# A decoder layer on one core: leading phase staggered by one pair, last third sum on VectorE, odd partial sums added from PSUM

## The chip, the core and the metric

The kernel runs on one core of a Trainium2 chip. Five engines work side by side, each through its own instructions in order: TensorE (PE, matrix products), VectorE (DVE), ScalarE (ACT), GpSimd (POOL) and SyncE (SP, which here only issues transfers). Transfers (DMAs) are issued by an engine's queue and carried out by 16 DMA engines that all queues share. SBUF is the working memory, PSUM holds the matmuls' sums. The metric is the time of one execution in microseconds; lower is better.

## The reference

One decoder layer for 256 tokens of width 2048, all in float32: a half-step SwiGLU feed-forward block, a mixing block (differential attention beside an mLSTM, between one input and one output projection), a second half-step feed-forward block and a final norm. The feed-forward block is the part that the change touches most:

```python
def swiglu(h, w_gate, w_up, w_down):
    return (jax.nn.silu(h @ w_gate) * (h @ w_up)) @ w_down

x = x + 0.5 * swiglu(rmsnorm(x, ffn1_norm[l]), ffn1_w_gate[l], ffn1_w_up[l], ffn1_w_down[l])
...
x = x + jnp.concatenate([y_a, y_b], axis=-1) @ w_out[l]
x = x + 0.5 * swiglu(rmsnorm(x, ffn2_norm[l]), ffn2_w_gate[l], ffn2_w_up[l], ffn2_w_down[l])
```

The hidden width is 5632, that is 11 column blocks of 512.

## The kernel before

**Splitting.** Each float32 operand is split into a high and a low half of TensorE's own format: ACT casts the high half (`wh`, L131), VectorE subtracts it from the source to get the low half (`wl`, L132). A product of two operands is three matmuls: high by high, low by high (L178, L179), high by low (L181). Each weight is loaded, split on both engines, and used by TensorE. The tiles of split weights come from a pool of four, so ACT and VectorE can be up to four tiles ahead of TensorE.

**Sums in place of products.** Two weight matrices that share their input (gate and up, or two column blocks of a projection) run as one `Paired` run. For its first `ns` pairs of row blocks it uses a scheme of the Strassen-Winograd kind, seven products in place of eight, in which sums of weight blocks are multiplied by sums of input blocks. For each pair `j` a tile `raw` with three slots is loaded: slot 0 from the first matrix, slots 1 and 2 from the second (`load`, L412 to L421, two DMAs on POOL's queue, on SP's for the first runs). There are five such tiles. The rest of the rows (`rest`) is done plainly, in units of two row blocks (`plain`, 12 matmuls each).

A run has these phases:
- `leading` (L440): for each group of up to two pairs (`twos`), load; multiply slot 0 by A1 into bank `x`; then one VectorE instruction of 1024 columns makes two sums in place (L453); multiply the new slot 0 by S1 into bank `d`; then add slot 2 to slot 0, the third sum. The third sum is an accumulating DMA on POOL's queue (L460) in runs with `by_dma` set and more than three pairs, else a VectorE instruction (L462). The bank `x` is copied to the bank n11 by ACT (L469) behind the last A1.
- `sums` (L487): multiply the third sums (S2) into `x`; for each of them a second block of the first matrix (`late`) is loaded and added to slot 0 by an accumulating DMA (L496), and is multiplied by itself (`bare`); then S3.
- `second` (L522): the plain units of the first matrix and the products of the remaining sums; it ends the first result (`half`).
- `third` (L541): the plain units of the second matrix. It is a stream, taken by the next run during its `leading`; behind its last unit stands `end`, the use of the second result.

**Order.** `Chain.run` (L566) interleaves by hand: with three steps of the stream and three groups it takes a unit, the first group, a unit, the second group, the third group, the last unit, and then `end`. TensorE's order follows this. Splits, sums and loads are moved ahead by a priority (`AHEAD`), and the instructions that drain PSUM are placed at most a few splits later by `ahead_of_splits`.

**Feed-forward.** The hidden columns are done in parts of 3, 2, 3 and 3 blocks (`PARTS`). For each part come its up/gate runs (five pairs each, but for the first two runs of the kernel), then the down projection over the part's rows, as two runs, for column blocks (0, 1) and (2, 3), with 3, 1, 3, 3 pairs (`NP_DOWN`). For every part but the last the result is a partial sum that is added to the residual `xres`: `add(c)` (L615) calls `add_part` (L324), in which ACT scales it out of PSUM into a tile (L329) and POOL issues an accumulating DMA into `xres` (L330). Even `c` comes from `second`, odd `c` from `third`, whose `end` stands in the next run's leading phase. For the last part and for the output projection `residual` adds from PSUM on VectorE (L336).

In the notation used below, A01 is the A1 product of pairs 0 and 1, S23 the S1 product of pairs 2 and 3, A4 and S4 those of the single pair 4, and U1 to U3 the units of the stream.

Of the kernel before, what the change touches and what calls it, by code (L numbers as in the profile page):

```python
# [13 lines left out]
ALU = mybir.AluOpType  # L14
# [6 lines left out]
NT = S // P  # L21
# [3 lines left out]
CW = 512  # L25
# [17 lines left out]
AHEAD = 400  # L43
# [4 lines left out]
SLACK = 4  # L48
# [11 lines left out]
def tile_trunk_layer(ctx: ExitStack, tc: tile.TileContext, x, xt, par, bias_if, lamv, fnorm,  # L60
                     wg1, wu1, wd1, wqk0, wqk1, wqk2, win, wout, wg2, wu2, wd2, out):
    nc = tc.nc
# [14 lines left out]
    def nm(s):  # L77
        uid[0] += 1
        return f"{s}_{uid[0]}"
# [16 lines left out]
    def seeded(which):  # L96
        return ps_acc.tile([P, CW], F32, tag=f"acc{which}", name=nm(f"acc{which}"), bufs=1)
# [24 lines left out]
    xres = big.tile([P, NT, D], F32, name="xres")  # L122
# [21 lines left out]
    def ahead_of_splits(i, ins, slack=SLACK):  # L144
        queued[i].append((len(splits) + slack, ins))
# [154 lines left out]
    A1, B1, A2, B2, S3, S1, S2, S4 = range(8)  # L300
# [24 lines left out]
    def add_part(acc, hb, c):  # L325

        t = wk("part")
        with soon():
            ahead_of_splits(0, nc.scalar.activation(t, acc, AF.Copy, scale=0.5))  # L329
        nc.gpsimd.dma_start(xres[:, hb, c * CW:(c + 1) * CW], t, accum_op=ALU.add)  # L330

    def residual(accs, c, scale, parts):
        for hb in range(NT):
            xs = xres[:, hb, c * CW:(c + 1) * CW]
            with soon():
                ahead_of_splits(1, nc.vector.scalar_tensor_tensor(xs, accs[hb], scale, xs, op0=ALU.mult, op1=ALU.add))  # L336
        for hb in range(NT):
            square_sum(xres[:, hb, c * CW:(c + 1) * CW], parts[:, hb, c:c + 1])

# [18 lines left out]
    def wk(name):  # L358
        return work.tile([P, CW], F32, tag="w", name=nm(name))
# [11 lines left out]
    def soon(extra=40):  # L371
        return tc.high_priority(offset=AHEAD + extra)
# [17 lines left out]
    def aside(work):  # L390

        if work:
            work.pop(0)()

    class Paired:
# [44 lines left out]
        def leading(self):  # L440

            n = self.n
            self.x, self.d = bank()[:, 0:n], bank()[:, 0:n]
            for js in self.twos:
                for j in js:
                    self.load(j)
                self.part(js, self.x, A1, 0, True, True)
                if js[-1] == self.ns - 1:
                    self.n11 = self.copied(self.x, seeded(N11), SLACK - 2)
                with tc.high_priority(offset=AHEAD):  # L450
                    for j in js:
                        raw = self.raws[j]
                        nc.vector.tensor_tensor(out=raw[:, 0:2, :], in0=raw[:, 0:3:2, :],  # L453
                                                in1=raw[:, 1:2, :].to_broadcast([P, 2, n]), op=ALU.add)
                self.part(js, self.d, S1, 0, True, True)
                with tc.high_priority(offset=AHEAD):
                    for j in js:
                        raw = self.raws[j]
                        if self.by_dma:
                            nc.gpsimd.dma_start(raw[:, 0, :], raw[:, 2, :], accum_op=ALU.add)  # L460
                        else:
                            nc.vector.tensor_tensor(out=raw[:, 0, :], in0=raw[:, 0, :], in1=raw[:, 2, :], op=ALU.add)  # L462
                yield

        def copied(self, src, t, slack=SLACK - 1):

# [91 lines left out]
    class Chain:  # L558
# [7 lines left out]
        def run(self, p, half, end, last_units=1, lead=()):  # L566

            done = 0
            for f in lead:
                next(self.stream)  # L570
                done += 1
                f()
            q = len(p.twos)
            first = p.leading()
            for i in range(q):
                while done < min(self.steps - 1, -(-(i + 1) * self.steps // (q + 1))):
                    next(self.stream)
                    done += 1
                next(first)
                flush(1)  # L580
                aside(side)
            while done < self.steps:
                next(self.stream)
                done += 1
            next(first, None)
            self.end()
            p.sums()
            half(p.second())
            self.put(p.third(last_units), len(p.rest), lambda: end(p.accs()))
# [7 lines left out]
    def ffn(chain, xp, rstd, wg, wu, wd, finish, first=None):  # L597


        def inner(hid, c, ns):  # L600
            sg = []

            def half(ag):
                r = rstd()
                sg.extend(gate(ag[hb], r[:, hb:hb + 1]) for hb in range(NT))

            def end(au):
                r = rstd()
                with soon():
                    hs = [gated(au[hb], r[:, hb:hb + 1], sg[hb]) for hb in range(NT)]  # L610
                hid_transposes(hs, hid, c, ns)

            return half, end

        def add(c):  # L615
            return lambda accs: [add_part(accs[hb], hb, c) for hb in range(NT)]

        done = 0
        for part, (n, ns) in enumerate(zip(PARTS, NP_DOWN)):
            hid = {}  # L620
            for c in range(n):
                half, end = inner(hid, c, ns)
                if done + c == 0 and first is not None:
                    half(linear(xp, wg[0], KD, ahead=first[0], in_pieces=True,
                                banks=[functools.partial(seeded, b) for b in (N11, N21)]))
                    au = []
                    stream = units(au, xp, wu[0], KD, banks=[bank, bank])
                    for _ in range(KD // UK - NP):
                        next(stream)
                    chain.put(stream, NP, functools.partial(end, au))  # L630
                else:
                    np_, queue = NP, nc.sync if done + c < ON_POOL else nc.gpsimd
                    if done + c == 1 and first is not None:
                        np_ = NP_FIRST
                        pending.extend([first[1]] * (NP - NP_FIRST))
                    chain.run(Paired(xp, wg[done + c], wu[done + c], KD, np_, queue=queue), half, end)
            last = part == len(PARTS) - 1
            for c in (0, 2):
                p = Paired(hid, wd[c], wd[c + 1], n * 4, ns, done, by_dma=False)
                if last:  # L640
                    chain.run(p, functools.partial(finish, c), functools.partial(finish, c + 1),
                              LAST_UNITS if c else 1)
                else:
                    chain.run(p, add(c), add(c + 1))
            done += n
# [158 lines left out]
    accs = []  # L804
# [182 lines left out]
    for hb in range(NT):  # L987
        for h in range(NH):
            i = hb * NH + h
# [226 lines left out]
```

## Time and profile before

| | |
|---|---|
| median of 3 runs | 1792.17 us (1791.81 to 1792.82) |
| the profiled execution | 1793.79 us |
| its span, first to last instruction | 1792.1 us |
| granted TensorE clock | 0.998 |
| instructions | 24444 |
| VectorE, ACT, POOL busy | 1565.1, 1255.2, 456.2 us |
| accumulating DMAs: third sums L460, late L496, partial sums L330 | 112, 168, 48 |

A row of the table of groups reads: line, engine, operation, out<-in by tile names, shapes, count | busy us, mean ns of one | idle us of the engine just before them, and what ended most of it. A row of the table of stages reads: the stretch in us from the span's start and its length, then for each engine its busy us with the number of its instructions in brackets, then the granted clock, the mean busy share of the 16 DMA engines, and GB/s moved. A row of the timeline reads: start, duration, engine, line, operation, tiles, shapes, count [idle before <-what ended it]. A row of the waits reads: who waited on what: total us, times, longest us. DMA rows of the timeline show the issue, not the transfer.

### The profile page before, as it was taken

What the parts mean: (1) busy time and instruction counts of PE and PEld (TensorE: products, weight loads), DVE (VectorE), ACT (ScalarE), POOL (GpSimd) and SP (SyncE); (2) the same over time, 40 slices, a digit from 0 to 9 for tenths busy, and PEclk for the clock granted to TensorE, in tenths of its full rate; (3) what the DMA queues carried; (4) which work ended last, traced back from release to release, by engine and by line L of the source; (5) the groups of instructions that cost most, each with busy time, mean ns of one, the idle gap of its engine ahead of it and who ended that gap; (6) DMA issues with size and microseconds to landing.
All of it is one profiled execution on the core that took longest, in us unless ns stands there. A gap on an engine that the chain in (4) does not pass through costs nothing.

```text
span 1792.1 us, 24444 instructions
## 1 busy us (share of the span) xinstructions
PE 1768.2 (99%) x7954; PEld 1437.8 (80%) x7954; DVE 1565.1 (87%) x2090; ACT 1255.2 (70%) x1939; POOL 456.2 (25%) x653
## 2 busy tenths in 40 slices
PE   9999999999999999999999999999999999999997
PEld 6788878878887888987788788788878878887886
DVE  6888887899888999897788998998887899888997
ACT  7676666777676768776676777776776777676765
POOL 0022332333233321022221102132332333233310
PEclk9999999999999999999999999999999999999999
DMA  9887998999799986587776568997998999899974
GB/s 339 263 239 211 263 284 252 238 307 255 235 261 267 261 267 193 189 247 211 217 217 202 179 197 231 257 279 217 260 283 261 239 304 246 249 257 271 273 255 123
DMA packets 159552, 439.15 MB, mean 245 GB/s; under 512 B 18016, under 2 KB 19072, under 8 KB 159168
## 3 DMA queue, kind: packets, MB, share of 16 engines
q0 software_dynamic: 79952, 200.60, 46.6%
q1 hardware_dynamic: 78464, 234.90, 38.0%
q10 hardware_dynamic: 1008, 2.09, 0.3%
q8 instruction: 62, 1.02, 0.2%
q14 instruction: 66, 0.54, 0.1%
HBM read 349.56 MB, written 2.10 MB: 196 GB/s over the span
## 4 chain that ended last, share of the span: by engine, by line
PE 82%; DMA 6%; issue 4%; DVE 4%; ACT 2%; POOL 1%; SPq 0%; POOLq 0%; DVEq 0%; ACTq 0%
PE acc L181 16%; PE acc L178 15%; PE acc L179 15%; PE accn L178 11%; PE accn L179 11%; PE accn L181 11%; DMA raw<-in_wg_dram 4%; DVE wl L132 2%; DMA rawp<-in_wg_dram 1%; ACT wh L131 1%; DVE raw L453 1%; PE tr L346 1%; DMA raw<-raw 1%; POOL raw L460 0%; PE sc L1008 0%
## 5 line engine op out<-in xcount | busy, mean ns | idle before, releaser
L131 ACT CAST wh<-raw 128x512 fp32r<-128x512 f32 (+1 forms) x845 | 570.7, 707 | 269.8 <-DVE raw L453 156.1
L132 DVE TENSOR_TENSOR wl<-raw,wh 128x512 fp32r<-128x512 f32 (+1 forms) x845 | 646.0, 792 | 122.8 <-ACT wh L131 118.2
L132 DVE TENSOR_TENSOR wl<-rawp,wh 128x1024 fp32r<-128x1024 f32 (+3 forms) x324 | 384.2, 1198 | 49.2 <-ACT wh L131 43.7
L131 ACT CAST wh<-rawp 128x1024 fp32r<-128x1024 f32 (+3 forms) x324 | 330.1, 1034 | 64.0 <-PE accn L179 22.9
L178 PE MATMUL acc<-wh,xs 128*128 128x512 f32 (+2 forms) x904 | 351.8, 390 | 6.7 <-ACT wh L131 6.7
L179 PE MATMUL acc<-wh,xs 128*128 128x512 f32 (+2 forms) x904 | 349.6, 387 | 0.6 <-DVE xs L132 0.6
L181 PE MATMUL acc<-wl,xs 128*128 128x512 f32 (+2 forms) x904 | 305.4, 390 | 1.6 <-DVE wl L132 1.4
L496 POOL DMA_DIRECT2D raw<-late x168 | 150.5, 1032 | 390.6 <-DVE wl L132 340.3
L178 PE MATMUL acc<-wh,xt 128*128 128x512 f32 (+2 forms) x608 | 235.5, 388 | 0.4 <-ACT wh L131 0.4
L179 PE MATMUL acc<-wh,xt 128*128 128x512 f32 (+2 forms) x608 | 233.8, 386 | 0.0
L178 PE MATMUL accn<-wh,xt 128*128 128x512 f32 (+1 forms) x592 | 233.3, 398 | 0.0
L179 PE MATMUL accn<-wh,xt 128*128 128x512 f32 (+1 forms) x592 | 228.8, 390 | 0.0
L178 PEld LDWEIGHTS acc<-wh,xs 128*128 128x128 f32 x904 | 169.8, 188 | 45.6 <-ACT wh L131 11.8
L181 PEld LDWEIGHTS acc<-wl,xs 128*128 128x128 f32 x904 | 168.7, 188 | 46.4 <-DVE wl L132 12.4
L453 DVE TENSOR_TENSOR raw<-raw 128x1024 f32<-128x1024 f32 x168 | 199.8, 1216 | 2.1 <-DMA raw<-in_wu_dram 1.6
L179 PEld LDWEIGHTS acc<-wh,xs 128*128 128x128 f32 x904 | 169.8, 188 | 34.6 <-DVE xs L132 1.8
L460 POOL DMA_DIRECT2D raw<-raw x112 | 96.5, 864 | 328.3 <-DVE wl L132 286.6
L181 PE MATMUL acc<-wl,xt 128*128 128x512 f32 (+2 forms) x608 | 171.6, 390 | 0.5
L181 PE MATMUL accn<-wl,xt 128*128 128x512 f32 (+1 forms) x592 | 166.3, 389 | 0.0
L178 PE MATMUL accn<-wh,xs 128*128 128x512 f32 (+1 forms) x384 | 150.1, 392 | 2.4 <-ACT wh L131 2.4
L179 PE MATMUL accn<-wh,xs 128*128 128x512 f32 (+1 forms) x384 | 149.0, 389 | 0.0
L181 PEld LDWEIGHTS acc<-wl,xt 128*128 128x128 f32 x608 | 111.3, 188 | 30.0 <-DVE wl L132 9.0
(231 smaller groups left out, 2164.8 us busy)
## 6 DMA issues: line engine op xcount, KB each, us to landing
rawp<-in_wd_dram SPq DMA_DIRECT2D x96, 512.0 KB, 5.7
raw<-late POOLq DMA_DIRECT2D x166, 256.0 KB, 5.1
raw<-in_wu_dram POOLq DMA_DIRECT2D x80, 512.0 KB, 8.7
rawp<-in_wu_dram SPq DMA_DIRECT2D x74, 512.0 KB, 5.8
rawp<-in_wg_dram SPq DMA_DIRECT2D x70, 512.0 KB, 5.6
raw<-raw POOLq DMA_DIRECT2D x112, 256.0 KB, 4.6
rawp<-in_win_dram SPq DMA_DIRECT2D x44, 512.0 KB, 5.1
late<-in_wg_dram SPq DMA_DIRECT2D x41, 512.0 KB, 10.5
```

The costliest lines, as they stand in the source:

```text
L131: return (nc.scalar.copy(hi, src), nc.vector.tensor_tensor(out=lo, in0=src, in1=hi.bitcast(F32), op=ALU.subtract))
L132: nc.vector.tensor_tensor(out=lo, in0=src, in1=hi.bitcast(F32), op=ALU.subtract))
L178: nc.tensor.matmul(acc, lh, rh, start=first, stop=False, skip_group_check=on)
L179: nc.tensor.matmul(acc, ll, rh, start=False, stop=False, skip_group_check=on)
L181: nc.tensor.matmul(acc, lh, rl, start=False, stop=last, skip_group_check=on)
L346: nc.tensor.transpose(tr[:, i, hb * P:(hb + 1) * P], hs[hb][:, k * P:(k + 1) * P], ident)
L453: nc.vector.tensor_tensor(out=raw[:, 0:2, :], in0=raw[:, 0:3:2, :], in1=raw[:, 1:2, :].to_broadcast([P, 2, n]), op=ALU.add)
L460: nc.gpsimd.dma_start(raw[:, 0, :], raw[:, 2, :], accum_op=ALU.add)
L496: nc.gpsimd.dma_start(self.raws[j][:, 0, :], lates[-1][1][:, i, :], accum_op=ALU.add)
```

## The change

Three things are done.

The leading phase is staggered. In the pass of a group, A1 is multiplied and the two sums are made as before, but the S1 product and the third sum (`second_sum`) are those of the group before. The last group's follow when the generator is asked once more. `Chain.run` asks for that before the last step of the stream, where it asked after it.

In runs whose third sums are DMAs, those of the last group are VectorE instructions.

The partial sums of odd `c` are added to `xres` by VectorE straight from PSUM (`add_half`, taken out of `residual`); those of even `c` go by ACT and DMA as before.

```diff
+    def add_half(acc, xs, scale):
+        with soon():
+            ahead_of_splits(1, nc.vector.scalar_tensor_tensor(xs, acc, scale, xs, op0=ALU.mult, op1=ALU.add))
+
     def residual(accs, c, scale, parts):
         for hb in range(NT):
-            xs = xres[:, hb, c * CW:(c + 1) * CW]
-            with soon():
-                ahead_of_splits(1, nc.vector.scalar_tensor_tensor(xs, accs[hb], scale, xs, op0=ALU.mult, op1=ALU.add))
+            add_half(accs[hb], xres[:, hb, c * CW:(c + 1) * CW], scale)
...
-            for js in self.twos:
+            for i, js in enumerate(self.twos):
                 for j in js:
                     self.load(j)
                 self.part(js, self.x, A1, 0, True, True)
-                if js[-1] == self.ns - 1:
-                    self.n11 = self.copied(self.x, seeded(N11), SLACK - 2)
...
-                self.part(js, self.d, S1, 0, True, True)
-                with tc.high_priority(offset=AHEAD):
-                    for j in js:
-                        raw = self.raws[j]
-                        if self.by_dma:
-                            nc.gpsimd.dma_start(raw[:, 0, :], raw[:, 2, :], accum_op=ALU.add)
-                        else:
-                            nc.vector.tensor_tensor(out=raw[:, 0, :], in0=raw[:, 0, :], in1=raw[:, 2, :], op=ALU.add)
+                if i:
+                    self.second_sum(self.twos[i - 1])
+                if i == len(self.twos) - 1:
+                    self.n11 = self.copied(self.x, seeded(N11), SLACK - 2)
                 yield
+            self.second_sum(self.twos[-1])
+
+        def second_sum(self, js):
+
+            self.part(js, self.d, S1, 0, True, True)
+            with tc.high_priority(offset=AHEAD):
+                for j in js:
+                    raw = self.raws[j]
+                    if self.by_dma and js != self.twos[-1]:
+                        nc.gpsimd.dma_start(raw[:, 0, :], raw[:, 2, :], accum_op=ALU.add)
+                    else:
+                        nc.vector.tensor_tensor(out=raw[:, 0, :], in0=raw[:, 0, :], in1=raw[:, 2, :], op=ALU.add)
...
+            while done < self.steps - 1:
+                next(self.stream)
+                done += 1
+            next(first, None)
             while done < self.steps:
                 next(self.stream)
                 done += 1
-            next(first, None)
             self.end()
...
         def add(c):
-            return lambda accs: [add_part(accs[hb], hb, c) for hb in range(NT)]
+            def run(accs):
+                for hb in range(NT):
+                    if c % 2:
+                        add_half(accs[hb], xres[:, hb, c * CW:(c + 1) * CW], 0.5)
+                    else:
+                        add_part(accs[hb], hb, c)
+
+            return run
```

## The prediction, made before the changed kernel was run

> **What bounds the kernel now.** I read the page first, its engine shares and DMA queues, then the table of stages, then the timeline of single stretches.
>
> ```profile
> PE 1768.2 (99%) x7954; PEld 1437.8 (80%) x7954; DVE 1565.1 (87%) x2090; ACT 1255.2 (70%) x1939; POOL 456.2 (25%) x653
> DMA  9887998999799986587776568997998999899974
> q0 software_dynamic: 79952, 200.60, 46.6%
> q1 hardware_dynamic: 78464, 234.90, 38.0%
> ```
>
> PE looks full at 99%, VectorE has 227 us free, and the two DMA queues together hold 84.6% of the 16 engines. But a matmul is drawn longer than the step to the next one (0.40 us in a row below, against 0.22), so PE's busy share hides small stalls. The count of matmuls in windows of one length shows them. Here are nine windows of 18 us, each ending where the leading phase of an up/gate run ends: six in the second run after a change of part, then three in the third run, or in the second one after the output projection.
>
> ```profile
> core 0: us, PE busy (x) PEld busy (x) DVE busy (x) ACT busy (x) POOL busy (x), PEclk, DMA share, GB/s
> 230.30:248.30 18.00, 16.99 (x72) 12.74 (x71) 14.91 (x18) 8.91 (x14) 4.52 (x6) 1.00 1.03 343
> 357.40:375.40 18.00, 17.16 (x73) 12.91 (x72) 15.23 (x18) 9.18 (x14) 4.52 (x6) 1.00 1.05 358
> 547.20:565.20 18.00, 15.84 (x66) 11.54 (x64) 13.60 (x17) 7.79 (x14) 3.87 (x5) 1.00 0.98 315
> 1307.10:1325.10 18.00, 17.36 (x75) 13.37 (x73) 15.51 (x18) 9.42 (x15) 6.09 (x9) 1.00 1.04 348
> 1433.70:1451.70 18.00, 17.37 (x76) 13.38 (x74) 15.61 (x18) 9.35 (x14) 4.58 (x7) 1.00 1.04 350
> 1621.80:1639.80 18.00, 17.01 (x73) 12.84 (x71) 14.99 (x18) 8.93 (x14) 4.53 (x6) 1.00 1.02 338
> 399.20:417.20 18.00, 18.00 (x81) 14.61 (x79) 16.70 (x21) 10.70 (x17) 5.58 (x8) 1.00 0.92 285
> 589.50:607.50 18.00, 17.66 (x78) 14.00 (x76) 16.22 (x20) 10.19 (x16) 5.60 (x8) 1.00 0.93 287
> 1118.30:1136.30 18.00, 17.70 (x77) 14.00 (x75) 15.47 (x18) 10.71 (x16) 3.48 (x4) 1.00 0.88 267
> ```
>
> A full window holds 81 matmuls, one every 18.00/81 = 0.222 us. The first six hold 72, 73, 66, 75, 76 and 73: 9+8+15+6+5+8 = 51 are missing, 51 x 0.222 = 11.3 us. In these six VectorE is not full either (13.6 to 15.6 us of 18), but the DMA engines are (0.98 to 1.05, against 0.88 to 0.93 in the three below). So two things are late there: data, and the chain of small steps. The first stretch shows both.
>
> ```profile
> ACT wh L131 <- DVE raw L453: 5.7, 3, 2.3
> DVE wl L132 <- ACT wh L131: 4.3, 5, 1.8
> ACT wh L131 <- DMA raw<-in_wg_dram: 3.1, 2, 2.1
> 246.47 0.40 PE L181 MATMUL acc<-wl,xs 128*128 128x512 f32 x1
> 247.50 0.50 PE L178 MATMUL acc<-wh,xs 128*128 128x512 f32 x1 [0.64 <-ACT wh L131]
> ```
>
> The first three rows are waits inside 230:249. ACT waits 3.1 us for the gate weights, and 5.7 us for the sums that VectorE makes of a pair (L453), because S1 is split straight after the sum it needs; VectorE in turn waits 4.3 us for ACT. The last rows are the end of this phase: PE starts S1 of pair 4 1.03 us after the last product of A1, where 0.22 would do.
>
> **The change, part by part.** Prices first.
>
> ```profile
> L462 DVE TENSOR_TENSOR raw<-raw 128x512 f32<-128x512 f32 x54 | 36.3, 688 | 0.8
> L453 DVE TENSOR_TENSOR raw<-raw 128x1024 f32<-128x1024 f32 x166 | 198.0, 1219 | 2.1 <-DMA raw<-in_wu_dram 1.6
> L336 DVE SCALAR_TENSOR_TENSOR xres<-acc,xres 128x512 f32<-128x512 f32 x8 | 5.5, 686 | 0.2 <-PE acc L181 0.2
> L329 ACT ACTIVATE part<-acc 128x512 f32<-128x512 f32 x24 | 14.3, 596 | 0.4
> L330 POOL DMA_DIRECT2D xres<-part x48 | 50.4, 1277 | 48.9 <-ACT part L329 48.4 <-issue 0.6
> L460 POOL DMA_DIRECT2D raw<-raw x112: 850/859/1107, 83.9 to 1681.8; - x112
> DMA to landing us min/median/max: 3.3/4.6/9.2
> ```
>
> (1) *Stagger.* No matmul, cast or sum is added or taken away. PE's order goes from U1, A01, S01, U2, A23, S23, A4, S4, U3 to U1, A01, U2, A23, S01, A4, S23, S4, U3 (U is a unit of the run before with 12 matmuls, 12 x 0.222 = 2.7 us; A and S of two pairs have 6, 1.3 us; of one, 3, 0.67 us). The chain from A's low half over the sum (1.22 us) and ACT's cast to S had no cover for S01, and now has U2 and A23, 4.0 us; S4 has S23, 1.3 us, which is more than the 0.8 us by which it was late. The copy of n11 on ACT (L469) is asked for after S23 now and must precede S2: it has S23, S4 and U3, 4.7 us. SP's queue keeps its loads in their order; POOL's gets L460 later (rival b). In the first paired run, with a single group, S01 came directly after A01; now one more unit stands between:
>
> ```profile
> 48.52 0.61 PE L181 MATMUL acc<-wl,xs 128*128 128x512 f32 x2
> 50.39 0.50 PE L178 MATMUL acc<-wh,xs 128*128 128x512 f32 x1 [1.25 <-ACT wh L131]
> ```
>
> The two matmuls of 48.52 make room for the next at 48.96; it starts at 50.39, 1.4 us late. That goes: **-1.4 us**.
>
> (2) *Third sum of the last pair on VectorE.* By the loops: 20 up/gate runs with five pairs give one each, three projection runs with four give two: 26 more of the L462 row (26 x 0.688 = 17.9 us on VectorE), 26 fewer L460 (86 stay). Of L460 the last one has the shortest time before its use in S2, and that landing is gone.
>
> (3) *Half of the partial sums from PSUM.* 24 fewer L329 (14.3 us of ACT, which has 7 us or more free in each of the nine windows: worth nothing by itself), 24 fewer L330, 24 more of the L336 kind: 24 x 0.686 = 16.5 us on VectorE. What is behind them in VectorE's order are splits; the change puts them where ACT's copy stood, up to four splits later. PSUM's banks come free about 0.1 us later, and are wanted a whole run later.
>
> What (2) and (3) take from the DMA engines: 24 + 26 = 50 transfers of 256 KB out of 328 accumulating ones (112 + 168 + 48). No row has their engine time, so I bound it. POOL's queue moved 200.60 MB, 328 x 0.262 = 86 MB of it accumulates and 114.6 MB loads. If these loads ran at the rate of the other queue (38.0% x 1792 / 234.9 = 2.9 us per MB), they took 332 us, which leaves 46.6% x 1792 - 332 = 503 us: 1.53 us for one. At the loads' own rate it would be 0.76 us. I take 1.53, since all-accumulate stretches run at about 200 GB/s with the engines full, against 340 above:
>
> ```profile
> 248.30:262.10 13.80, 13.72 (x59) 11.04 (x60) 13.33 (x19) 11.40 (x19) 5.22 (x6) 1.00 0.99 209
> ```
>
> The place matters more than the total. Before the first stalled window POOL's queue reads:
>
> ```profile
> 205.83 0.86 POOL L460 DMA_DIRECT2D raw<-raw  x1 [1.72 <-DVE wl L132]
> 211.23 2.10 POOL L330 DMA_DIRECT2D xres<-part  x2
> 213.13 1.09 POOL L496 DMA_DIRECT2D raw<-late  x1
> 222.84 0.57 POOL L418 DMA_DIRECT2D raw<-in_wg_dram  x1 [8.62 <-DVE wl L132]
> ```
>
> The L330 pair is the odd column group (c = 3) of the down projection before; the L460 is a last pair. All three go, 3 x 1.53 = 4.6 us of DMA time ahead of the late loads. On average a stalled window lacks 11.3/6 = 1.9 us, at most 15 x 0.222 = 3.3. So here stagger and freed DMA time each cover most of the stall by themselves. I leave a remainder of 1.5 matmuls in each window, between the 0 and the 3 to 4 that the last three windows lack: 6 x 1.5 x 0.222 = 2.0 us. **-9.3 us**. Those last windows' own 3 and 4 missing ones (1.6 us) go by half: **-0.8 us**.
>
> By the Trainium skill's page "DMA: Bandwidth & Descriptors", section Where 436 GB/s comes from, an SBUF-to-SBUF transfer is bound by the fabric, 435 GB/s: an estimate of 0.60 us for 256 KB, and 1.8 us instead of 4.6 before each window, less than the average stall. The stretch at 209 GB/s speaks against that here.
>
> *The cost.* VectorE gets 50 more instructions, 34.4 us, 1565 to 1599 us or 89%. In the stalled windows it has 2.4 us or more free; in the tight ones 1.3 (16.70 of 18) to 2.5 us, for one more of 0.69. The two adds of c = 3 fall behind the lead of the first run of a part. So the work fits; in order, it can still push S2's first splits. Bounds: nothing, or all 20 third sums, 13.8 us. I take 0.7 us, near the idle that the L462 row shows around 54 such instructions (0.8 us): **+0.7 us**.
>
> The page "SBUF — State Buffer", section Who interferes with whom, of the Trainium skill says that a VectorE instruction with two SBUF inputs contends with a GpSimd instruction that reads SBUF, so 26 more third sums could hold up POOL's issues by up to one duration each. The L460 row shows issues of 850 to 1107 ns, median 859, beside a VectorE that is busy 87% of the time: no such hold-up is seen.
>
> Sum: -9.3 - 1.4 - 0.8 + 0.7 = **-10.8 us**. The profiled execution took 1793.79 us around its span of 1792.1; that gives 1783.0. It stood 1.6 us above the median 1792.17, so the forecast is **1781.4 us**.
>
> **Rivals.** *(a) VectorE eats most of it.* For: it is the only engine that gains work, and the three last windows have it at 15.5 to 16.7 us of 18 with PE just served. Against: the stagger takes away its own waits for ACT. If half of the 20 third sums (6.9 us) reach PE, the time is 1781.4 - 0.7 + 6.9 = 1787.6, at the edge of no change. If all of them do (13.8), it is 1794.5.
>
> *(b) Slower: S2 waits for third sums that now start later.* S01 is split behind U2 and A23 with their sums, S23 behind A4 and its sum, so the remaining L460 issue later, by VectorE work of 1.2 + 1.2 + 2.4 = 4.8 us for pairs 0 and 1 and of 0.7 + 1.2 = 1.9 us for 2 and 3. In the tight lead:
>
> ```profile
> 414.75 0.85 POOL L460 DMA_DIRECT2D raw<-raw  x1 [0.35 <-DVE wl L132]
> 418.15 2.18 ACT L131 CAST wh<-raw 128x512 fp32r<-128x512 f32 x4
> ```
>
> Pair 3 is issued at 414.75 and cast fourth, at about 419.7: 5.0 us. With 1.9 taken off, and 0.7 given by the third sum ahead of S2, some 3.8 us stay, against landings of 3.3 to 9.2, median 4.6. The cast is made ahead of PE's need by the split buffers, about 1 us, which is why I do not expect a stall. It decides if landings are above 4.8 us. At 5.8, each of 20 runs loses 1 us: 1781.4 + 20 = 1801.
>
> *(c) More than forecast.* All of the leading stalls go, and the split phases behind them (59 matmuls in 13.8 us in the row above, 62 would fit; some 0.5 us in 20 runs) gain too: 1781.4 - 2.8 - 10 = 1769.
>
> **How the numbers follow.** Forecast 0.58, (a) 0.22, (b) 0.12, (c) 0.08. About 0.2% (3.6 us) is what a measurement of this kernel can tell from no change: 1788.6 to 1795.8. Half of (a) lies in it: same 0.12 with a little of (b)'s mild end; faster 0.58 + 0.11 + 0.08 = 0.77; slower 0.11. The range leaves out the far end of (b) and of (c): 1770 to 1794.
>
> **What would show it.** Right: 81 or so matmuls in the six windows, DMA share below 1 there; VectorE near 1599 us with 2140 instructions; L460 x86, L330 x24. Wrong: ACT waiting for raw<-raw before S2 (b), or VectorE above 17.5 us in the leads with PE waiting for L132 (a). The forecast fails if the planner puts the second sums elsewhere than the loops say.

## The result, and the profile after

| | before | after |
|---|---|---|
| median of 4 runs | 1792.49 us | 1780.56 us (1779.92 to 1781.01) |
| span of the profiled execution | 1792.1 us | 1778.5 us |
| ratio, 95% interval | | 0.9933 [0.9916, 0.995] |

The change makes the kernel 12 us faster; 1781.4 was forecast. The page of the kernel after, in the lines shown of before:

```profile
PE 1759.8 (99%) x7954; PEld 1441.8 (81%) x7954; DVE 1590.0 (89%) x2140; ACT 1258.9 (71%) x1915; POOL 413.5 (23%) x603
...
DMA  9787997999799876586776577897998999798974
...
q0 software_dynamic: 72752, 187.49, 42.3%
q1 hardware_dynamic: 78464, 234.90, 38.8%
```

PE is at 99% in both, as before: the share says nothing of 12 us. The DMA queues fell from 84.6% of 1792.1 us to 81.1% of 1778.5, that is by 1516.1 - 1442.4 = 73.7 us, or 1.47 us for each of the 50 transfers that went.

The table of stages of the kernel after, for the six stalled leading phases (18 us each, ending at the copy of n11):

```profile
core 0: us, PE busy (x) PEld busy (x) DVE busy (x) ACT busy (x) POOL busy (x), PEclk, DMA share, GB/s
228.40:246.40 18.00, 18.00 (x81) 14.93 (x80) 16.18 (x20) 11.21 (x17) 5.67 (x9) 1.00 0.89 288
353.30:371.30 18.00, 18.00 (x81) 14.92 (x80) 15.89 (x20) 11.15 (x16) 5.27 (x9) 1.00 0.84 287
539.10:557.10 18.00, 18.00 (x81) 14.93 (x80) 16.18 (x20) 11.11 (x17) 5.67 (x9) 1.00 0.97 331
1298.30:1316.30 18.00, 18.00 (x81) 14.90 (x80) 16.12 (x20) 11.23 (x16) 5.55 (x9) 1.00 0.89 292
1422.90:1440.90 18.00, 18.00 (x81) 14.89 (x81) 16.17 (x20) 11.12 (x16) 5.91 (x9) 1.00 0.89 289
1609.50:1627.50 18.00, 18.00 (x81) 14.67 (x79) 15.59 (x19) 10.58 (x16) 5.47 (x8) 1.00 0.87 283
```

All six are full: 81 matmuls where there were 66 to 76, with a DMA share of 0.84 to 0.97 in place of 0.98 to 1.05. So are the three other leads that were counted before the change (81, 78 and 77 then):

```profile
393.80:411.80 18.00, 18.00 (x81) 14.93 (x80) 17.75 (x23) 11.46 (x17) 5.58 (x9) 1.00 0.84 285
579.60:597.60 18.00, 18.00 (x82) 14.88 (x81) 17.69 (x23) 11.59 (x18) 5.52 (x9) 1.00 0.84 283
1110.50:1128.50 18.00, 18.00 (x81) 14.90 (x80) 15.35 (x18) 11.56 (x17) 1.76 (x2) 1.00 0.77 252
```

To see where else time came or went, one needs a place of the work that both kernels have. The product of gate and up on VectorE (`sg`, L368 before, L370 after) nearly is one: it ends a block of hidden columns, inside the next run's leading phase. Some of its rows in the timeline of VectorE, before:

```profile
58.51 0.74 DVE L368 SCALAR_TENSOR_TENSOR sg<-acc,rstd,sg 128x512 f32<-128x512 f32 x1
...
252.37 0.74 DVE L368 SCALAR_TENSOR_TENSOR sg<-acc,rstd,sg 128x512 f32<-128x512 f32 x1
...
649.79 0.74 DVE L368 SCALAR_TENSOR_TENSOR sg<-acc,rstd,sg 128x512 f32<-128x512 f32 x1
...
1140.26 1.52 DVE L368 SCALAR_TENSOR_TENSOR sg<-acc,rstd,sg 128x512 f32<-128x512 f32 x2
```

and after:

```profile
57.38 0.75 DVE L370 SCALAR_TENSOR_TENSOR sg<-acc,rstd,sg 128x512 f32<-128x512 f32 x1
...
251.21 0.75 DVE L370 SCALAR_TENSOR_TENSOR sg<-acc,rstd,sg 128x512 f32<-128x512 f32 x1
...
641.36 0.75 DVE L370 SCALAR_TENSOR_TENSOR sg<-acc,rstd,sg 128x512 f32<-128x512 f32 x1
...
1133.86 1.41 DVE L370 SCALAR_TENSOR_TENSOR sg<-acc,rstd,sg 128x512 f32<-128x512 f32 x2
```

Read them as a race. At the first of these rows the new kernel is 58.51 - 57.38 = 1.1 us ahead, at 252.37 it is 1.2 ahead, at 649.79 it is 8.4 ahead, and behind the mixing block and the output projection (1140.26) only 6.4: **2.0 us are lost there**. But the row is only nearly the same place: 208 matmuls of weights (L178, L179 and L181) have started before the row of 58.51, and 204 before that of 57.38, a difference of 4 x 0.227 = 0.9 us. So the table below counts these matmuls instead; every trace has 7464 of them. A stretch lies between the same two counts in both kernels, and the figure is by how many microseconds the new kernel gets through it sooner than the kernel before. The columns behind the first are kernels of the experiments; "fastest" is the last but one of the section on what the change loses.

| stretch, with its times in the kernel before | after | stagger only | adds only | adds + third | after, first output run plain | fastest |
|---|---|---|---|---|---|---|
| up to the 100th of these matmuls (31.98) | -1.4 | -0.3 | 0.2 | -0.7 | 0.0 | 0.5 |
| from there to the third block (144.06) | 0.3 | -1.0 | 0.0 | 0.0 | -0.8 | 0.0 |
| the six stalled leads (the windows of the prediction) | 12.4 | 12.3 | 10.7 | 12.0 | 12.3 | 11.3 |
| the split phases right behind these six | 1.2 | -2.2 | 0.1 | 0.5 | -0.1 | 1.0 |
| mixing and output projection (649.79 to 1140.26) | -1.6 | -2.6 | -0.4 | 1.5 | 2.3 | 2.6 |
| the rest | 2.6 | -5.5 | 1.9 | 0.7 | 2.4 | 2.8 |
| whole span | 13.6 | 0.8 | 12.5 | 14.0 | 16.1 | 18.3 |

This is one profiled execution of each kernel, so some of it is chance. The first row shows how much: the first paired run has not begun there, and yet the kernel after is 1.4 us behind. PE waits longer for the cast of its first weights, before and after:

```profile
9.58 0.50 PE L178 MATMUL accn<-wh,xs 128*128 128x512 f32 x1 [1.67 <-ACT wh L131]
```

```profile
10.08 0.50 PE L178 MATMUL accn<-wh,xs 128*128 128x512 f32 x1 [3.26 <-ACT wh L131]
```

Over all kernels of this document the first row of the table lies between -1.9 and 1.0. The gain is where it was forecast, in the six leads (12.4 us); the loss in the output projection lies where none was.

### The profile page after: what moved, and what is told of

It is laid out like the page before. It is cut to its first block, busy times and chain, and to the rows that moved or that the text cites. A ratio compares the mean times of both kernels' runs of the same rounds, so it can differ in the third digit from the quotient of the medians.

```text
span 1778.5 us, 24397 instructions
## 1 busy us (share of the span) xinstructions
PE 1759.8 (99%) x7954; PEld 1441.8 (81%) x7954; DVE 1590.0 (89%) x2140; ACT 1258.9 (71%) x1915; POOL 413.5 (23%) x603
## 3 DMA queue, kind: packets, MB, share of 16 engines
q0 software_dynamic: 72752, 187.49, 42.3%
## 5 line engine op out<-in xcount | busy, mean ns | idle before, releaser
L178 PE MATMUL acc<-wh,xs 128*128 128x512 f32 (+2 forms) x904 | 350.9, 389 | 1.4 <-ACT xs L131 0.7
L179 PE MATMUL acc<-wh,xs 128*128 128x512 f32 (+2 forms) x904 | 349.3, 387 | 0.5 <-DVE xs L132 0.5
L181 PE MATMUL acc<-wl,xs 128*128 128x512 f32 (+2 forms) x904 | 302.4, 388 | 1.1 <-DVE wl L132 1.0
L178 PE MATMUL acc<-wh,xt 128*128 128x512 f32 (+2 forms) x608 | 235.3, 388 | 0.1
L179 PE MATMUL acc<-wh,xt 128*128 128x512 f32 (+2 forms) x608 | 233.4, 385 | 0.0
L178 PE MATMUL accn<-wh,xt 128*128 128x512 f32 (+1 forms) x592 | 233.4, 397 | 0.0
L179 PE MATMUL accn<-wh,xt 128*128 128x512 f32 (+1 forms) x592 | 229.7, 391 | 0.5
L178 PEld LDWEIGHTS acc<-wh,xs 128*128 128x128 f32 x904 | 169.7, 188 | 38.0 <-ACT us L477 1.9
L181 PEld LDWEIGHTS acc<-wl,xs 128*128 128x128 f32 x904 | 168.7, 188 | 38.5 <-DVE wl L132 4.8
L179 PEld LDWEIGHTS acc<-wh,xs 128*128 128x128 f32 x904 | 169.8, 188 | 34.2 <-DVE xs L132 1.0
L181 PE MATMUL acc<-wl,xt 128*128 128x512 f32 (+2 forms) x608 | 169.3, 387 | 0.7 <-DVE wl L132 0.4
L181 PE MATMUL accn<-wl,xt 128*128 128x512 f32 (+1 forms) x592 | 165.9, 388 | 0.0
L178 PE MATMUL accn<-wh,xs 128*128 128x512 f32 (+1 forms) x384 | 150.5, 393 | 4.3 <-ACT wh L131 4.2
L179 PE MATMUL accn<-wh,xs 128*128 128x512 f32 (+1 forms) x384 | 149.3, 390 | 0.0
L469 POOL DMA_DIRECT2D raw<-raw x86 | 74.7, 896 | 311.0 <-DVE wl L132 290.2
L178 PEld LDWEIGHTS accn<-wh,xt 128*128 128x128 f32 x592 | 110.4, 188 | 29.8 <-ACT accn L477 7.3
```

The lines of the kernel that those rows point to most:

```text
L178: nc.tensor.matmul(acc, lh, rh, start=first, stop=False, skip_group_check=on)
L179: nc.tensor.matmul(acc, ll, rh, start=False, stop=False, skip_group_check=on)
L181: nc.tensor.matmul(acc, lh, rl, start=False, stop=last, skip_group_check=on)
```

## The experiments

Theory: the leads stalled because late loads met full DMA engines and because S1 stood straight behind its own sum; stagger and freed DMA time each lift that by themselves. Rivals: only one of the two does; the stagger moves the wait to S2 (rival b); VectorE eats part of the gain (rival a). Each kernel was timed in five rounds against the kernel before on the same chip: the first four beside 1793.09 us, the next four beside 1793.67, the last four beside 1793.63. Edits are shown against the kernel after; "stagger off" is this one, with the copy of n11 and the end of the leading phase where they stood before:

```diff
-                if i:
-                    self.second_sum(self.twos[i - 1])
+                self.second_sum(js)
...
-            self.second_sum(self.twos[-1])
```

### The parts alone

**Stagger only.** Third sums and partial sums are all DMAs again.

```diff
-                    if self.by_dma and js != self.twos[-1]:
+                    if self.by_dma:
...
-                    if c % 2:
-                        add_half(accs[hb], xres[:, hb, c * CW:(c + 1) * CW], 0.5)
-                    else:
-                        add_part(accs[hb], hb, c)
+                    add_part(accs[hb], hb, c)
```

> The leading phase is staggered; all third sums and all partial sums are DMAs as before, so the DMA load is that of before. Theory of the prediction (stagger and freed DMA time each cover the six stalled leads by themselves): the six leads hold 78 or more matmuls in 18 us with the DMA engines still full, and the time is 1783 to 1787 us. Rival 'only late data': the leads still lack 5 to 15 matmuls, 1789 or more. Rival 'only the stagger counts': all of the gain, 1780 to 1781. If third sums of the last group now land late, ACT waits for raw<-raw before S2 and some of the gain is given back.

Measured: 1794.56 us, ratio 1.0008 [0.9999, 1.0016]: no gain. Yet the leads are full. Stages of this kernel, the first and the third of the six, and the split phase behind the second:

```profile
229.80:247.80 18.00, 18.00 (x81) 14.93 (x80) 16.09 (x19) 10.90 (x16) 6.26 (x10) 1.00 0.91 304
...
546.10:564.10 18.00, 18.00 (x81) 14.93 (x80) 16.04 (x19) 11.22 (x17) 5.98 (x9) 1.00 0.92 301
...
374.60:390.00 15.40, 14.12 (x58) 10.39 (x58) 12.60 (x18) 11.31 (x19) 5.41 (x7) 1.00 0.99 212
```

ACT's waits for third sums (waiter, what it waited on: total us, times, longest) in the kernel before, in this one and in the kernel after:

```profile
ACT wh L131 <- DMA raw<-raw: 4.1, 7, 2.4
```

```profile
ACT wh L131 <- DMA raw<-raw: 35.4, 38, 3.6
```

```profile
ACT wh L131 <- DMA raw<-raw: 10.9, 22, 1.8
```

They rise from 4.1 us to 35.4 with the stagger alone. The split phase holds 58 matmuls where 15.40/0.222 = 69 would fit, and ACT waits there for a third sum (raw<-raw) up to 3.6 us. So the stagger alone lifts the stall in the leads and hands it to S2: rival (b) is real, and it takes most of the gain. By the count of matmuls the six leads win 12.3 us, and the split phases of all 45 paired runs lose 9.6, where those of the kernel after win 1.1. The whole change is late in the output projection too, so a part of the 9.6 has the cause shown there. The DMA engines were expected to be still full in the leads; they are at 0.90 to 0.94.

**Adds only.** Stagger off, third sums all DMAs; odd partial sums from PSUM.

```diff
-                    if self.by_dma and js != self.twos[-1]:
+                    if self.by_dma:
```

> Only the odd partial sums are added from PSUM by VectorE; leading phase and third sums as before. Theory of the prediction: the DMA time freed before the late loads (2 x 1.5 us) brings the six leads from 66 to 76 matmuls to 76 to 79, 1784 to 1788 us. Rival 'only late data': 1781 to 1784. Rival 'only the stagger counts': leads as before, 1791 to 1793.

Measured: 1781.29 us, 0.9934 [0.9921, 0.9946]: as much as the whole change, and the time that the rival "only late data" gave, not the 1784 to 1788 of the prediction's theory. Its stages, the first, third and last lead:

```profile
228.00:246.00 18.00, 18.00 (x81) 14.81 (x80) 15.47 (x18) 10.27 (x16) 5.59 (x8) 1.00 0.96 294
...
539.80:557.80 18.00, 18.00 (x81) 14.77 (x80) 15.52 (x18) 10.46 (x16) 5.59 (x8) 1.00 0.99 317
...
1611.00:1629.00 18.00, 17.52 (x76) 13.65 (x75) 15.52 (x18) 9.49 (x16) 4.61 (x7) 1.00 0.96 300
```

The six hold 81, 79, 81, 81, 81 and 76: without any stagger, 44 of the 51 missing matmuls are back.

**Last third sum only.** Stagger off, all partial sums by DMA (the second half of the first diff).

> Only the third sums of the last group are VectorE instructions; no stagger, partial sums by DMA. Theory of the prediction: 26 transfers fewer, of which one (1.5 us) stands before each stalled lead, against 17.9 us more of VectorE work in the densest stretch: 1789 to 1793 us, S2 of the last pair never waits for a landing. Rival 'VectorE is the bound': 1795 or more.

Measured: 1788.73 us, 0.9977 [0.9966, 0.9987]: 4 us, just below the range expected. Its six leads hold 68 to 78 matmuls: 12 of the 51 are back. The third of its leads shows that the engines are still full and the stall still there:

```profile
546.50:564.50 18.00, 16.39 (x68) 11.89 (x67) 14.30 (x18) 8.39 (x13) 4.44 (x6) 1.00 1.03 335
```

### Is it the DMA time?

Adds only takes away 24 transfers and ACT's copies ahead of them, and adds 24 instructions on VectorE. The control gives the transfers and copies back and keeps the adds: ACT copies the sum times zero, and POOL adds these zeros to the same part of `xres`, so the result is unchanged.

```diff
-    def add_part(acc, hb, c):
+    def add_part(acc, hb, c, scale=0.5):
...
-            ahead_of_splits(0, nc.scalar.activation(t, acc, AF.Copy, scale=0.5))
+            ahead_of_splits(0, nc.scalar.activation(t, acc, AF.Copy, scale=scale))
...
                         add_half(accs[hb], xres[:, hb, c * CW:(c + 1) * CW], 0.5)
+                        add_part(accs[hb], hb, c, 0.0)
```

> As e2 (odd partial sums added by VectorE from PSUM), but ACT also copies each of them out of PSUM times zero and POOL adds that tile of zeros to the same part of the residual by the old accumulating DMA: VectorE's new work without the freed DMA time. Theory (the freed DMA time makes the gain of e2): the six leads lack matmuls as before, 1791 to 1794 us. Rival (the gain of e2 comes from the order of the instructions or from a sum that is ready sooner): 1781 to 1784 us.

Measured: 1793.05 us, 0.9995 [0.9987, 1.0004]. The gain is gone. Its stages, first, third and last lead:

```profile
233.00:251.00 18.00, 17.09 (x74) 13.12 (x72) 15.19 (x18) 9.19 (x15) 4.53 (x6) 1.00 0.99 321
...
547.60:565.60 18.00, 17.36 (x76) 13.61 (x74) 15.61 (x18) 9.51 (x15) 4.93 (x7) 1.00 1.02 333
...
1620.20:1638.20 18.00, 17.30 (x74) 13.22 (x73) 15.35 (x18) 9.45 (x15) 4.55 (x7) 1.00 0.99 324
```

The time is that of the kernel before again, so the gain hangs on the copies and transfers, and the 24 adds on VectorE cost nothing that can be measured. In the leads only about half of the stall is back: the six hold 74, 75, 76, 77, 80 and 74, so 30 matmuls are missing where 7 are with adds only and 51 were before. Where the profiled execution loses what its leads still win (4.8 us by the count of matmuls) is clear only in part: 1.9 us are lost before the 100th matmul, by chance. The control does not part the copy from its transfer either. ACT had 7 us or more free in each of these windows, and the DMA share of the six is 0.98 to 1.05, against 0.96 to 0.99 with adds only; that speaks for the transfer, and does not show it.

**All partial sums from PSUM, no stagger.** If each transfer were worth the same, the other 24 would bring as much again.

```diff
-                    if c % 2:
+                    if True:
```

> Old order of the leading phase, all third sums as before, all 48 partial sums added by VectorE from PSUM. Theory (the odd ones stand right ahead of the late loads, the even ones do not): no more than 2 us from e2, 1779 to 1783 us. Rival (the total of DMA time counts): 4 us or more below e2.

Measured: 1781.53 us, 0.9932 [0.992, 0.9944], the same as with the odd ones alone, as the theory had it. So the second 24 are worth nothing once the first are gone. Whether that is their place, or only that the leads were nearly full by then (44 of 51), is not shown: the even ones were not taken away alone, and in the kernel before those of `c` = 2 leave with the engines full as well (a DMA share of 1.07 in the 12 us behind the first of them, 190.8).

### The parts in pairs

**Stagger and last third sum**, all partial sums by DMA (second half of the first diff).

> Stagger and last third sum on VectorE, all partial sums by DMA. Theory: e1 lost its gain in part to S2, which waited for third sums that land late; with the last group's on VectorE the DMAs left land sooner and about 4 us of these waits go, while the 4 us in the output projection stay: 1785 to 1789 us. Rival (those waits come from VectorE's backlog): 1794 or more.

Measured: 1782.0 us, 0.9934 [0.9921, 0.9946], better than expected: the third sum on VectorE, worth 4 us alone, is worth 13 on top of the stagger. The wait that had taken the stagger's gain shrinks from 35.4 us in 38 to:

```profile
ACT wh L131 <- DMA raw<-raw: 12.4, 24, 1.4
```

**Adds and last third sum**, stagger off.

> Both reliefs of the DMA engines, no stagger. Theory (the stagger is not needed for the gain): 1777 to 1780 us, the six leads at 78 or more matmuls. Rival (the last third sum on VectorE needs the stagger, or VectorE is full): 1782 or more.

Measured: 1781.28 us, 0.993 [0.9917, 0.9942], 1 us above the range expected, and the same as adds alone. Its leads are full (12.0 us won in the table, against 10.7 with adds only), and yet the time is the same; what takes the difference was not isolated.

So three of these kernels, and the whole change, all come to 0.993: the reliefs are not additive, since each lifts the same stall.

### What the change loses

**First output-projection run in the old order**, all else as after.

```diff
+            self.stagger = stagger
...
-                if i:
+                if not self.stagger:
+                    self.second_sum(js)
+                elif i:
                     self.second_sum(self.twos[i - 1])
...
-        chain.run(Paired(yT, wout[c], wout[c + 1], KD, NP_OUT), functools.partial(finish_out, c),
+        chain.run(Paired(yT, wout[c], wout[c + 1], KD, NP_OUT, stagger=c > 0), functools.partial(finish_out, c),
```

> The changed kernel, but the first run of the output projection keeps the old order of its leading phase (S1 of a group right behind its A1). In the changed kernel PE stands still about 4 us more there than before. Theory: the stagger asks there for A2 before S01, and A2's input is made late by the transposes of the mixing block, so PE waits; undone there, 1776 to 1778 us. Rival: the wait comes from VectorE's extra work or from the transposes alone, no change, 1780 to 1781.

Measured: 1775.9 us, 0.9904 [0.989, 0.9917], 0.1 us below the range expected. The place is another one than expected: the stall of the kernel after lies not at A2 and S01 but in the split phase behind them. That phase in the stages before, after, and of this kernel:

```profile
1002.80:1013.60 10.80, 10.80 (x51) 8.66 (x50) 10.76 (x19) 9.93 (x18) 2.69 (x3) 1.00 0.70 161
```

```profile
994.80:1009.40 14.60, 12.55 (x55) 8.25 (x54) 12.76 (x25) 12.87 (x25) 2.70 (x3) 1.00 0.64 155
```

```profile
995.60:1006.50 10.90, 10.90 (x53) 8.65 (x51) 10.86 (x19) 9.96 (x18) 2.69 (x3) 1.00 0.69 156
```

It takes 14.6 us in place of 10.8, for 55 matmuls in place of 51, with 25 instructions on VectorE and on ACT in place of 19 and 18. What has come in are the mixing block's last outputs (L385, `xt<-tr,prm`), inputs of this projection: eight instructions on each of the two engines. In the old order they come behind this phase, with the stagger inside it. The first of VectorE's, in the kernel after and in this one:

```profile
1000.54 0.87 DVE L385 SCALAR_TENSOR_TENSOR xt<-tr,prm,xt 128x256 fp32r<-128x256 f32 x2
```

```profile
1008.80 0.48 DVE L385 SCALAR_TENSOR_TENSOR xt<-tr,prm,xt 128x256 fp32r<-128x256 f32 x1
```

So the new order does not meet an input that is late by itself; it draws the making of later inputs forward, in among the splits of this phase. PE's longest waits there in the kernel after are for a cast (`wh`, 0.7 us), for the low half of an input sum (`xs`, 0.5) and for the low half of a weight (`wl`, 0.5). Which of the 16 instructions delays them was not isolated.

**Stagger in runs of five pairs only**: the first runs and both output-projection runs in the old order.

```diff
+            self.stagger = ns > 4
```

> The whole change, with the stagger only in the runs of five pairs; all others keep the old order of the leading phase. Theory: the stagger costs 4 us in the output projection (as e4 showed) and 0.5 us in the lead of each of six down projections, and gains about 1 us in the first paired run: 1772 to 1776 us, below e4. Rival (the old order is late in other runs too): 1776 or more.

Measured: 1777.28 us, 0.9908 [0.9893, 0.9924]: 1 us above the range, as the rival had it. A stall that no other kernel has stands behind the output projection. Timelines of this kernel: POOL's third sums (here L475) and late sums (L510), ACT, PE; and the stage of the stall:

```profile
1079.95 1.75 POOL L475 DMA_DIRECT2D raw<-raw  x2 [5.89 <-DVE wl L132]
1083.21 2.67 POOL L510 DMA_DIRECT2D raw<-late  x3 [1.51 <-DVE wl L132]
```

```profile
1089.04 0.62 ACT L131 CAST wh<-raw 128x512 fp32r<-128x512 f32 x1 [4.55 <-DMA raw<-raw]
```

```profile
1089.71 0.50 PE L178 MATMUL acc<-wh,xs 128*128 128x512 f32 x1 [2.10 <-ACT wh L131]
```

```profile
1087.00:1090.00 3.00, 0.90 (x4) 0.48 (x3) 0.31 (x1) 0.96 (x2) 0.00 (x0) 1.00 1.08 198
```

The second third sum is issued at 1080.56 and has landed at 1089.02, 8.5 us later, just before its cast starts; three late sums are issued meanwhile, and the DMA share is 1.08. This is rival (b) with the long landing that it asked for.

**The same, with the second output-projection run staggered.**

```diff
-            self.stagger = ns > 4
+            self.stagger = stagger or ns > 4
...
+        chain.run(Paired(yT, wout[c], wout[c + 1], KD, NP_OUT, stagger=c > 0), functools.partial(finish_out, c),
```

> As e8 (stagger in the runs of five pairs alone), but the second run of the output projection is staggered too. In e8 PE stood still 4 us in the split phase of the first up/gate run behind the output projection, where e4, with that run staggered, did not. Theory (a staggered run behind one that is not, at that place, is late): the 4 us go, 1772 to 1774 us. Rival (e8's stall there has another cause): 1777.

Measured: 1774.72 us, 0.9892 [0.9879, 0.9906], 0.7 us above the range expected and the fastest of all: 18.9 us under the kernel before, and its interval lies below that of the change (0.9916 to 0.995).

**The same, with all partial sums from PSUM** (the `if True` above).

> As e9, and the even partial sums are added by VectorE from PSUM too: no accumulating DMA into the residual is left in the feed-forward blocks, VectorE gets 24 more instructions (16.5 us). Theory (freed DMA time is worth something only ahead of late loads, and those are on time now): within 2 us of e9. Rival (DMA time is still short): 3 us or more faster. Rival (VectorE is at its limit): 3 us or more slower.

Measured: 1775.42 us, 0.9897 [0.9883, 0.991]: no difference from the one above, as expected.

### The limit of VectorE

**All third sums on VectorE**, the rest as after: 86 more instructions and no L469.

```diff
-                    if self.by_dma and js != self.twos[-1]:
+                    if False:
```

> The whole change, and all third sums are VectorE instructions: 86 more of 0.69 us (59 us, VectorE at 93%), and no third sum by DMA. Theory (the leads of five pairs have 1.3 to 2.5 us of VectorE time to spare, this asks for 2.8): PE waits for VectorE, 1790 us or more. Rival (what counts is the DMA time and the landing, VectorE has room): 1781 or less.

Measured: 1806.23 us, 1.0069 [1.0055, 1.0083], slower than before. Its page, and its row of PE's waits for VectorE, with that of the kernel after below:

```profile
PE 1776.5 (98%) x7954; PEld 1436.2 (80%) x7954; DVE 1633.8 (91%) x2226; ACT 1255.9 (70%) x1915; POOL 338.5 (19%) x517
```

```profile
PE acc L181 <- DVE wl L132: 10.0, 17, 1.2
```

```profile
PE acc L181 <- DVE wl L132: 1.4, 3, 0.5
```

Rival (a) thus has its point: 26 third sums more on VectorE cost nothing that the times show, 112 do. It takes 26 us for 86, or 0.30 us each, although VectorE shows 9% idle. The place is the split phases, where VectorE has no time left. The one behind the first stalled lead, in the kernel after and in this one:

```profile
246.40:260.60 14.20, 14.20 (x65) 11.72 (x64) 14.17 (x20) 11.45 (x20) 4.49 (x6) 1.00 0.98 207
```

```profile
246.10:262.20 16.10, 16.07 (x73) 12.56 (x72) 16.10 (x24) 13.56 (x23) 4.40 (x5) 1.00 0.70 154
```

Added up over the split phases of all 45 paired runs, what the starts of PE's matmuls lie further apart than 0.227 us is 34.9 us here and 14.7 in the kernel after.

## Why the prediction was right, point by point

**The six leads (-9.3).** Right in place, a little small: all 51 missing matmuls came back, not 42, and the six leads won 12.4 us by the count of matmuls. The remainder of 1.5 matmuls in each window was too careful. That each relief covers most of this stall by itself was shown for the leads: stagger alone fills all six, adds alone bring 44 of 51. For the time it was wrong: stagger alone gains nothing.

**The price of an accumulating transfer (1.53 us).** It measured 1.47 us as a mean over 50, from both queues. POOL's queue alone lost 46.6% of 1792.1 - 42.3% of 1778.5 = 82.8 us, 1.66 for each, while SP's took 9.1 us more for the same bytes. That a transfer's place matters more than the number was shown: the 24 odd partial sums bring 12 us, the 26 third sums of the last groups 4, and the 24 even partial sums behind the odd ones nothing.

**The first paired run (-1.4).** The step failed in what follows it. The gap is gone (timeline of the kernel after; the next matmul starts 0.22 us after the second of the two):

```profile
49.92 0.61 PE L181 MATMUL acc<-wl,xs 128*128 128x512 f32 x2
50.37 0.39 PE L178 MATMUL acc<-wh,xt 128*128 128x512 f32 x1
```

But smaller stalls come in its place. From the 100th to the 430th matmul (31.98 to 109.74 before) the kernel after wins 0.3 us, and the four others with staggered first runs lose 0.2 to 1.0; the eight with the old order stand within 0.3 us of the kernel before.

**The other leads (-0.8).** Too careful as well: the three windows hold 81, 82 and 81, so all 7 missing matmuls (1.6 us) came back, not half of them. Where the rest of the span won its 2.6 us was not taken apart further.

**VectorE (+0.7).** No run shows this term by itself; the adds and the last third sums cost nothing that the times show clear of chance. The counts came as said (2140 instructions, L469 x86, L330 x24), the busy time did not: 1590 us, not 1599 (see the last section). The six windows have it at 15.6 to 16.2 us of 18, but in two of the three other leads it stands at 17.75 and 17.69, above the 17.5 that was to speak for rival (a). PE is served there all the same (81 and 82 matmuls), so only half of that sign came.

**Rival (b)** was given 0.12 as a thing that happens or does not. It happens in part: ACT's wait for third sums rose from 4.1 to 10.9 us in the change as made, to 12.4 without the third part of it, and to 35.4 without the second and the third. The prediction left some 3.8 us from issue to cast for the third sum of pair 3; the landings had a median of 3.7 us in the kernel after, and a longest of 7.3. It counted the last third sum as a DMA saved; its larger use is that it takes the latest landing away from S2. **Rival (a)** did not come with 26 more third sums on VectorE, and did with 112; where between them it begins was not tried.

**What was missed** is the output projection: 2.0 us by the `sg` rows, 1.6 by the count of matmuls, 4.7 by the time without it (1780.56 - 1775.9). The prediction counted 20 up/gate runs and did not ask what other work the new order would draw into the phases of this run.

So the total is right partly because misses cancel. In the six leads and the split phases behind them 12.4 + 1.2 us were won where 9.3 were forecast, and 2.6 in the rest where 0.8 were to be won and 0.7 lost; the first paired runs won 0.3 instead of 1.4, the output projection lost 1.6, and the start lost 1.4 by chance. Against the same profiled execution the change made 13.6 us, where 10.8 were forecast; the medians lie 1792.49 - 1780.56 = 11.9 us apart.

## What to carry to other kernels

When an engine shows 99%, count its instructions in equal windows; that shows where it stalls and whether a change fills the gap. Price a transfer by what waits behind it, not by its length: 24 transfers were worth 12 us, 26 others of the same size 4, and 24 more nothing once the first were gone. A reordering that covers one wait can delay the next user, so make that user's input earlier in the same change, and look at what other work it draws into a phase that had none to spare. Compare two kernels at equal counts of the work, since the same instruction need not stand at the same place of it.

## What was not expected of the hardware

The stall of the kernel with stagger in runs of five pairs only cost more than its own length. Its stages of 1 us, from the end of the stall on:

```profile
1090.00:1091.00 1.00, 1.00 (x5) 0.72 (x5) 1.00 (x3) 1.00 (x2) 0.32 (x1) 0.84 0.14 25
1091.00:1092.00 1.00, 1.00 (x4) 0.81 (x3) 1.00 (x1) 1.00 (x4) 0.54 (x1) 0.50 0.07 12
1092.00:1093.00 1.00, 1.00 (x4) 0.67 (x4) 1.00 (x3) 0.88 (x2) 0.00 (x0) 0.50 1.02 180
...
1094.00:1095.00 1.00, 1.00 (x6) 0.82 (x5) 1.00 (x3) 1.00 (x4) 0.47 (x1) 0.95 0.96 365
```

PE idles 2.1 us (the row of 1089.71 above); about 1 us after it has work again the granted clock is halved, for 0.32 + 3.00 + 0.10 = 3.4 us (from the shares 0.84, 0.50 and 0.95), which costs an estimated half of that, 1.7 us. The stalls of the kernel after in the output projection, in gaps of 0.7 us or less, left the clock at 1.00. The Trainium skill's page "TensorE: Matmul & The Clock Gate", Part 1: The HAM clock gate, has the clock at half rate behind an idle window of about 3.4 us, until one such window has been busy. The length of the slow stretch agrees; the idle time ahead of it was shorter here.

Idle time alone does not decide it. While the first weights are loaded, five of the fourteen profiled executions show the same 3.4 us at half rate: the kernel after behind the 3.26 us of idle PE shown above, and four more behind 1.79 to 3.78 us. The others do not, among them adds only with 2.38 us of idle PE and the kernel with the first output run plain with 2.24. What decides between them is not shown. A stretch of stagger with last third sum, behind 2.05 us:

```profile
10.00:13.10 3.10, 3.10 (x9) 2.42 (x8) 1.63 (x4) 2.10 (x2) 0.00 (x0) 0.50 1.02 414
```

An instruction of VectorE that is drawn 0.687 us long takes less of the engine, since neighbours overlap in the drawing (three of 0.69 in a row span 1.89 us, at 243.72 in the kernel before): 50 more raised its busy time by 1590.0 - 1565.1 = 24.9 us and 86 more by 1633.8 - 1590.0 = 43.8, 0.50 and 0.51 us each.
